# Seven block products for eight in a two-layer block's up projection, with the down projection as a stage of its own

## The chip, the core and the metric

The kernel runs on one core of one Trainium2 chip. The number that counts is the time of one execution in device microseconds (us). TensorE (PE) multiplies matrices, VectorE (DVE), ScalarE (ACT) and GpSimd (POOL) work elementwise, and SyncE (SP) issues most DMA transfers between DRAM and the on-chip memory SBUF. Each engine takes its instructions in order, so one that waits holds up all behind it. Matmul results land in PSUM, a small memory of eight banks.

## The reference

Two layers over 1024 tokens of width 1024, all in fp32. The change lies in the feed-forward part of the first, between its attention and the second layer:

```python
def conv_glu_ffn(h, w_up, w_conv, b_conv, w_down):
    z = h @ w_up                                   # 1024 x 1024 by 1024 x 5632
    zp = jnp.pad(z, ((0, 0), (1, 1), (0, 0)))      # three neighbouring tokens
    z = zp[:, :-2] * w_conv[0] + zp[:, 1:-1] * w_conv[1] + zp[:, 2:] * w_conv[2] + b_conv
    a, b = jnp.split(z, 2, axis=-1)                # 2816 channels each
    return (jax.nn.silu(a) * b) @ w_down           # 2816 x 1024
...
h = rmsnorm(x, g_norm2[l]) * (1.0 + sc2) + sh2
x = x + gt2 * conv_glu_ffn(h, w_up[l], w_conv[l], b_conv[l], w_down[l])
```

## The kernel before

Every fp32 product is made of three matmuls on a rounded type: a value is split into a high part (a cast on ACT) and a rest (a subtraction on DVE), and `mm3` multiplies high by high, rest by high and high by rest (L166 to L168 in the profile). `split` is that pair, with its lines L79 and L81.

The 2816 gated channels are 22 tiles of 128. Tile m has two weight tiles of `w_up`, one for `a` and one for `b`. `up_tile` multiplies one of them by all tokens: two halves of 512 tokens, eight blocks of 128 in the contracted width, three matmuls each, so 48 matmuls of 128x512 for a weight tile and 44 x 48 = 2112 in all. The result stays in PSUM (`up`), from where ACT (L1019) and two DVE instructions (L1020, L1022) make the three-token filter. ACT makes the SiLU of `a` (L1043), DVE the product with `b` (L1050), which is split into `gh` and `gl`. `down_w` loads the rows of `w_down` that belong to the tile, multiplies them by the gate row `gt2` on POOL (L992) and splits them.

After two such tiles `down` adds their part of the down projection: eight blocks of 128 tokens, two halves of 512 columns, 2 x 3 matmuls each, and a DVE addition into the rows `x2` (L1006). That is 96 matmuls for a group of two tiles and 11 x 96 = 1056 in all. `x2`, eight tiles of 512 KB, and `gt2` stay in SBUF throughout. The down groups are written in between the up tiles, so PE goes from one to the other. The next weight tile is loaded and split one tile ahead by `weights` and `w_next` along a list, `weight_order`, which runs on through the second layer.

In front of this the last two output-projection halves are interleaved with the normalised and transposed tokens 0 to 511 (`h_first`); `norm2(1)` and `to_act(xn[1], ...)` do the same for tokens 512 to 1023 while the first two up tiles multiply tokens 0 to 511. The transposed, split tokens are `h2T` (`h2h`, `h2l`). Behind it, `first_tokens` starts the second layer's input.

Of the kernel before, what the change touches and what calls it, by code (L numbers as in the profile page):

```python
# [6 lines left out]
F32 = mybir.dt.float32  # L7
# [289 lines left out]

def load_columns(cx, I):  # L300


# [30 lines left out]

def first_layer(cx, I, specs, x4_scr):
    nc = cx.nc
    tt = nc.vector.tensor_tensor
    ts = nc.vector.tensor_scalar
# [626 lines left out]
    def out_last():  # L966
        for n in range(2):
            yield from out_half(2 + n, ws[n], 1)
            if n == 0:
                cx.w_next()  # L970
                cx.w_next()
# [9 lines left out]
    wc = [cx.col["w_conv0"], cx.col["w_conv1"], cx.col["w_conv2"]]  # L981
    bc = cx.col["b_conv"]
    gt2 = gates[1]

    def down_w(m):
        hi = cx.pg("wdh", dt=F32R)
        lo = []
        for j in range(2):
            s = slice(j * 512, j * 512 + 512)
            f = cx.ge("wdf")  # L990
            nc.sync.dma_start(f, w_down[m * P:(m + 1) * P, s])
            nc.gpsimd.tensor_tensor(out=f, in0=f, in1=gt2[:, s], op=ALU.mult)  # L992
            lo.append(cx.hp("wdl", dt=F32R))
            cx.split(hi[:, s], lo[j], f)
        return hi, lo

    def down(gs, dws, rows=range(8), after=None):
        for i in rows:
# [12 lines left out]
    def up_tile(m, part):
        w = cx.weights(m > 0)
        c = m + NF * part
        S = cx.ps("S", "up", w=1024)
        for b in range(2):
            yield from cx.gemm_ch(S[:, b * 512:b * 512 + 512], h2T, w, b)
            yield 1.3
        y = cx.pg("y")
        nc.scalar.activation(y, S, AF.Identity, scale=wc[1][:, c:c + 1], bias=bc[:, c:c + 1])  # L1019
        stt(out=y[:, 1:], in0=S[:, :1023], scalar=wc[0][:, c:c + 1], in1=y[:, 1:],  # L1020
            op0=ALU.mult, op1=ALU.add)
        stt(out=y[:, :1023], in0=S[:, 1:], scalar=wc[2][:, c:c + 1], in1=y[:, :1023],  # L1022
            op0=ALU.mult, op1=ALU.add)
        return y

    def run(gen):
        while True:
            try:
                next(gen)
            except StopIteration as e:  # L1030
                return e.value

    pend_down, gs, dws = None, [], []
    for m in range(NF):
        ups = [up_tile(m, part) for part in range(2)]
        if m == 0:
            for u in ups:
                drain(half(u))
            drain(cx.to_act(xn[1], h2T, 1, a2, sh2))
        ya = run(ups[0])  # L1040
        if m == 0:
            cx.w_next()
        nc.scalar.activation(ya, ya, AF.Silu)  # L1043
        if pend_down is not None and m < NF - GRP:
            drain(down(*pend_down))
            pend_down = None
        yb = run(ups[1])
        if m == 0:
            cx.w_next()
        tt(out=ya, in0=ya, in1=yb, op=ALU.mult)  # L1050
        gs.append((cx.pg("gh", dt=F32R), cx.pg("gl", dt=F32R)))
        cx.split(*gs[-1], ya)
        dws.append(down_w(m))
        if len(gs) == GRP and m < NF - 1:
            pend_down, gs, dws = (gs, dws), [], []

# [821 lines left out]

def scratch(nc):
    d = lambda n, s: nc.dram_tensor(n, s, F32, kind="Internal").ap()  # L1880
    return {"x4": d("scr_x4", (1024, 1024)), "da": d("scr_da", (P, P)), "fc": d("scr_fc", (P, P)),
            "xs": d("scr_xs", (1024, 1024)), "ys": d("scr_ys", (1024, 1024)), "ya": d("scr_ya", (1024, 1024)),
            "t1": d("scr_t1", (1024, 1024)),
            "g0": d("scr_g0", (1024, 1024)), "g1": d("scr_g1", (1024, 1024))}


def weight_order(cx, I):

    w_in, w_in2 = I["w_in"][0], I["w_in_2"][0]
# [3 lines left out]
    order += [(I["w_out"][0], c, 256, "pg" if c % 512 else "wp") for c in range(0, 1024, 256)]  # L1893
    order += [(I["w_up"][0], (m + NF * part) * P, P, "wp") for m in range(NF)
              for part in range(2)]
    order += [(w_in2, c, 256, "wp", *what[1]) if kind == "v" else (w_in2, c, P, "wp")
              for kind, c, what in second_tasks()]
# [37 lines left out]
```

## Time and profile before

| | |
|---|---|
| three runs | 2695.33, 2696.01 (median), 2696.12 us |
| the profiled execution | 2694.87 us |
| its span, first to last instruction | 2693.0 us |
| up projection, first to last matmul start | 559.3 to 1239.2 us |
| down projection, first to last addition | 622.5 to 1293.1 us |

Busy time is a share of the span. The starts of matmuls, one after the other, tell PE's pace; the duration of one (389 ns) is longer, since neighbours overlap.

### The profile page before, as it was taken

What the parts mean: (1) busy time and instruction counts of PE and PEld (TensorE: products, weight loads), DVE (VectorE), ACT (ScalarE), POOL (GpSimd) and SP (SyncE); (2) the same over time, 40 slices, a digit from 0 to 9 for tenths busy, and PEclk for the clock granted to TensorE, in tenths of its full rate; (3) what the DMA queues carried; (4) which work ended last, traced back from release to release, by engine and by line L of the source; (5) the groups of instructions that cost most, each with busy time, mean ns of one, the idle gap of its engine ahead of it and who ended that gap; (6) DMA issues with size and microseconds to landing.
All of it is one profiled execution on the core that took longest, in us unless ns stands there. A gap on an engine that the chain in (4) does not pass through costs nothing. (4 is left out here: it accounts for less than half of the span.)

```text
span 2693.0 us, 38385 instructions
## 1 busy us (share of the span) xinstructions
PE 2626.4 (98%) x15391; PEld 2208.2 (82%) x15391; DVE 1547.2 (57%) x2857; ACT 1014.4 (38%) x1753; POOL 391.3 (15%) x368
## 2 busy tenths in 40 slices
PE   5999999999999999999899999999999999999999
PEld 5998667988888888887687777888888888888899
DVE  6645776665555555555577887554554544474443
ACT  4434776142222222223444444343343433352222
POOL 2211210431111111112202212310110100110000
PEclk9999999999999999999999999999999999999999
DMA  7111213421111111111123333222222222253532
GB/s 250 39 55 48 67 44 105 127 67 47 47 48 54 47 48 54 49 51 65 56 86 97 94 102 103 82 65 62 75 87 56 70 84 60 71 196 118 176 126 114
DMA packets 225439, 221.56 MB, mean 82 GB/s; under 512 B 15109, under 2 KB 173421, under 8 KB 225261
## 3 DMA queue, kind: packets, MB, share of 16 engines
q1 hardware_dynamic: 224608, 218.60, 26.4%
q8 instruction: 121, 1.98, 0.3%
q10 hardware_dynamic: 652, 0.51, 0.1%
q14 instruction: 58, 0.47, 0.1%
HBM read 180.67 MB, written 34.21 MB: 80 GB/s over the span
## 5 line engine op out<-in xcount | busy, mean ns | idle before, releaser
L81 DVE TENSOR_TENSOR wlo<-land,wh 128x1024 fp32r<-128x1024 f32 x161 | 209.1, 1300 | 323.5 <-ACT wh L79 322.7
L79 ACT CAST wh<-land 128x1024 fp32r<-128x1024 f32 x163 | 170.9, 1050 | 570.7 <-PE up L167 344.4
L166 PE MATMUL up<-h2h,wh 128*128 128x512 f32 x704 | 273.9, 390 | 0.7 <-DVE y L1022 0.7
L167 PE MATMUL up<-h2l,wh 128*128 128x512 f32 x704 | 274.1, 389 | 0.0
L168 PE MATMUL up<-h2h,wlo 128*128 128x512 f32 x704 | 273.9, 389 | 0.0
L1006 DVE TENSOR_TENSOR x<-dn,x 128x512 f32<-128x512 f32 x176 | 119.2, 688 | 75.5 <-PE dn L168 75.5
L1560 POOL TENSOR_TENSOR prob<-fc,consts 128x128 f32<-128x128 f32 x128 | 68.6, 555 | 635.1 <-PE pT L1600 278.3
L103 POOL TENSOR_TENSOR rstd<-ms,mhalf 128x1 f32<-128x1 f32 (+3 forms) x58 | 76.0, 1310 | 579.1 <-DVE ms L101 579.1
L89 ACT COPY pf<-pT 128x512 f32<-128x512 f32 (+1 forms) x208 | 114.0, 560 | 116.3 <-PE pT L1600 79.2
L166 PE MATMUL ag<-h3h,wh 128*128 128x512 f32 x384 | 156.9, 408 | 0.0
L992 POOL TENSOR_TENSOR wdf<-wdf,gate 128x512 f32<-128x512 f32 x44 | 73.4, 1690 | 568.5 <-DMA wdf<-in_w_down_dram 556.8
L166 PEld LDWEIGHTS up<-h2h,wh 128*128 128x128 f32 x704 | 132.1, 188 | 28.5 <-issue 1.1
L167 PEld LDWEIGHTS up<-h2l,wh 128*128 128x128 f32 x704 | 132.1, 188 | 27.7 <-DVE h2l L228 0.4
L168 PEld LDWEIGHTS up<-h2h,wlo 128*128 128x128 f32 x704 | 132.1, 188 | 27.5
L1580 ACT ACTIVATE prob<-prob,m 128x128 f32<-128x128 f32 (+7 forms) x128 | 99.4, 777 | 140.6 <-DVE m L1574 139.7
L168 PE MATMUL ag<-h3h,wlo 128*128 128x512 f32 x384 | 150.6, 392 | 0.0
L167 PE MATMUL ag<-h3l,wh 128*128 128x512 f32 x384 | 150.1, 391 | 0.0
L166 PE MATMUL dn<-wdh,gh 128*128 128x512 f32 x352 | 138.2, 393 | 1.7 <-DVE x L1006 1.5
L167 PE MATMUL dn<-wdl,gh 128*128 128x512 f32 x352 | 137.4, 390 | 0.0
L168 PE MATMUL dn<-wdh,gl 128*128 128x512 f32 x352 | 137.1, 389 | 0.0
L166 PE MATMUL tok<-wh,h1h 128*128 128x256 f32 x448 | 130.5, 291 | 2.7 <-ACT h1h L226 2.7
L168 PE MATMUL tok<-wh,h1l 128*128 128x256 f32 x448 | 128.7, 288 | 0.8 <-DVE h1l L228 0.8
(348 smaller groups left out, 6967.0 us busy)
## 6 DMA issues: line engine op xcount, KB each, us to landing
land<-in_w_in_dram SPq DMA_DIRECT2D x87, 512.0 KB, 4.0
wada<-in_w_ada_dram SPq DMA_DIRECT2D x96, 256.0 KB, 3.6
land<-in_w_up_dram SPq DMA_DIRECT2D x44, 512.0 KB, 3.9
wdf<-in_w_down_dram SPq DMA_DIRECT2D x44, 256.0 KB
scr_g<-gt SPq DMA_DIRECT2D x34, 256.0 KB, 3.5
x<-in_x_dram SPq DMA_DIRECT2D x16, 512.0 KB, 5.8
land<-in_w_out_dram SPq DMA_DIRECT2D x16, 512.0 KB
dab<-scr_da SPq DMA_DIRECT2D x32, 256.0 KB, 4.5
```

The costliest lines, as they stand in the source:

```text
L79: i = self.nc.scalar.copy(hi, src)
L81: eng.tensor_tensor(out=lo, in0=src, in1=hi.bitcast(F32), op=ALU.subtract)
L89: self.nc.scalar.copy(dst, src)
L103: self.nc.gpsimd.tensor_tensor(out=r[:, :width], in0=t[:, :width], in1=self.mhalf[:, :width], op=ALU.pow)
L166: i = mm(out, lh, rh, start=first, stop=False, **kw)
L167: mm(out, lh, rl, start=False, stop=False, **kw)
L168: self.last = mm(out, ll, rh, start=False, stop=last, **kw)
L992: nc.gpsimd.tensor_tensor(out=f, in0=f, in1=gt2[:, s], op=ALU.mult)
L1006: tt(out=x2[i][:, s], in0=o, in1=x2[i][:, s], op=ALU.add)
L1560: nc.gpsimd.tensor_tensor(out=pt[:, qs], in0=fc[:, qs], in1=cx.pos_q, op=ALU.add)
L1580: nc.scalar.activation(pt[:, :W], pt[:, :W], AF.Exp, bias=top, scale=-1.0, accum_out=rs)
```

## The change

The up projection of a pair of weight tiles (tile m of `a` and of `b`) is a product of a 2 x 2 matrix of blocks (two weight tiles by two halves of the contracted width) and another (the halves of that width by the two halves of the tokens). The class `Pairs` makes it of seven block products instead of eight. Each is 4 x 3 = 12 matmuls of 128x512, so a pair takes 84 instead of 96 and the stage 22 x 84 = 1848. For this POOL forms four sums of weight blocks in each pair (`sums`), ACT and DVE split seven (`split`), and two copies on ACT and five additions on DVE put the products together (`take`), from PSUM into SBUF tiles `z`. The filter, now in `gated`, reads `z`. The sums of token blocks (`T1` to `T4`, `B22`) are formed once ahead of the loop by `blocks(k)`, k = 0 to 3, on ACT, DVE and POOL; only the four products of tiles 0 and 1 that need tokens 0 to 511 alone come before it.

The product `a * b` goes to DRAM (`scr["g"]`), and so do `x2` and `gt2` ahead of the stage. The down projection follows when the up projection is over: its pools reuse the memory, `x2` and `gt2` are loaded back, and `load_group` brings each group's gate products and `w_down` rows. Its matmuls are as many as before. PSUM is divided anew in each stage.

```diff
+SEVEN = [("A11", "B11", "X"), ("S2", "T2", "Y"), ("A12", "B21", "X"), ("S3", "T3", "Z"),
+         ("S1", "T1", "W"), ("-A22", "T4", "Z"), ("S4", "B22", "W")]
...
+    def step(self, n, j, z, between=lambda: None):
+        if j == 0:
+            self.load(n + 2)
+        self.product(n, j)
+        self.sums(n + 1, j)
+        self.split(n + 1, j)
+        between()
+        self.take(n, j, z)
...
-    norm2(1)
...
+        for e in range(2):
+            ts(out=xh[j, e], in0=x_[:, e * 512:e * 512 + 512], scalar1=r, scalar2=None,
+               op0=ALU.mult)
+    for i in range(8):
+        nc.sync.dma_start(scr["x2"][i * P:(i + 1) * P, :], x2[i])
+    nc.sync.dma_start(scr["gt2"], gates[1][0:1, :])
+    psum.close()
+    yield
...
+    def blocks(k):
+        f = cx.pg("bf", (P, 2, 512))
+        o = cx.pg("bo", (P, 2, 512))
+        for e in range(2):
+            kk_ = k + 4 * e
+            t = cx.ps("T", "tr")
+            for j in range(4):
+                nc.tensor.transpose(t[:, j * P:(j + 1) * P], xh[j, e][:, k * P:(k + 1) * P],
+                                    cx.ident)
+            nc.scalar.activation(f[:, e], t, AF.Identity, scale=a2[:, kk_:kk_ + 1],
+                                 bias=sh2[:, kk_:kk_ + 1])
+            h, l = h2T(kk_, 0)
+            nc.gpsimd.tensor_tensor(out=o[:, e], in0=h.bitcast(F32), in1=l.bitcast(F32),
+                                    op=ALU.add)
+        cx.split(*b_new("B22", k, 0), f[:, 1])
+        t1, t3 = cx.t("sf", "t1", (P, 512)), cx.t("sf", "t3", (P, 512))
+        tt(out=t1, in0=f[:, 0], in1=o[:, 0], op=ALU.subtract)
+        nc.gpsimd.tensor_tensor(out=t3, in0=f[:, 1], in1=f[:, 0], op=ALU.subtract)
+        t2 = f[:, 0]
+        tt(out=t2, in0=f[:, 1], in1=t1, op=ALU.subtract)
+        cx.split(*b_new("T2", k, 0), t2)
+        cx.split(*b_new("T3", k, 0), t3)
+        cx.split(*b_new("T1", k, 0), t1)
+        tt(out=o[:, 1], in0=t2, in1=o[:, 1], op=ALU.subtract)
+        cx.split(*b_new("T4", k, 0), o[:, 1])
...
+    for m in range(2):
+        for j in (0, 2):
+            up.product(m, j)
+            up.take(m, j, z_of(m))
...
+    for k in range(4):
+        blocks(k)
...
+        tt(out=y[0], in0=y[0], in1=y[1], op=ALU.mult)
+        nc.sync.dma_start(scr["g"][m * P:(m + 1) * P, :], y[0])
...
+    psum.enter_context(cx.psum("psd", S=2, T=3, V=1))
+    cx.plan(second_weights(cx, I))
+    gt2 = cx.pg("gate")
+    cx.bcast_row(gt2, scr["gt2"][0])
+    x2 = []
+    for i in range(8):
+        t = cx.pg("x2")
+        nc.sync.dma_start(t, scr["x2"][i * P:(i + 1) * P, :])
+        x2.append(t)
...
+    def load_group(q):
+        g, w = [], []
+        for m in range(GRP * q, GRP * q + GRP):
+            gh, gl = cx.pg("gh", dt=F32R), cx.pg("gl", dt=F32R)
+            nc.sync.dma_start(gl.bitcast(F32), scr["g"][m * P:(m + 1) * P, :])
...
+                nc.sync.dma_start(f, w_down[m * P:(m + 1) * P, j * 512:j * 512 + 512])
...
+    for q in range(1, NF // GRP - 1):
+        gen = group(q)
+        drain(down(*cur, range(0, 3)))
+        nxt = next(gen)
+        drain(down(*cur, range(3, 8)))
```

Three places where the order of instructions differs. SP at the start of the stage, before (weight tiles of the up projection follow those of the output projection, `land`; `wada` are weights of the modulation):

```order
L125 DMA land_5443<-in_w_out_dram 128x4x256
L125 DMA land_5445<-in_w_out_dram 128x4x256
L362 DMA wada_5574<-in_w_ada_dram 128x512
L125 DMA land_5597<-in_w_up_dram 128x8x128
L125 DMA land_5978<-in_w_up_dram 128x8x128
L125 DMA land_5984<-in_w_up_dram 128x8x128
```

and after (`scr_gt` and `scr_x` are the stores of `gt2` and `x2`, `pairs` the raw weights of one pair, two transfers of 512 KB):

```order
L473 DMA wada_5577<-in_w_ada_dram 128x512
L1098 DMA scr_gt<-gate_5421 1x1024
L1097 DMA scr_x<-x_975_4557 128x1024
L1097 DMA scr_x<-x_976_4559 128x1024
L1097 DMA scr_x<-x_977_4561 128x1024
L1097 DMA scr_x<-x_978_4563 128x1024
L1097 DMA scr_x<-x_1077_4928 128x1024
L1097 DMA scr_x<-x_1078_4930 128x1024
L1097 DMA scr_x<-x_1079_4932 128x1024
L1097 DMA scr_x<-x_1080_4934 128x1024
L323 DMA pairs_6233<-in_w_up_dram 128x8x128 x2
L323 DMA pairs_6236<-in_w_up_dram 128x8x128 x2
```

The first `w_up` weights now stand on SP behind all eight stores of `x2`.

SP at the end of the up projection, before (weights of up and down in turn):

```order
L991 DMA wdf_10050<-in_w_down_dram 128x512
L991 DMA wdf_10181<-in_w_down_dram 128x512
L125 DMA land_9795<-in_w_up_dram 128x8x128
L125 DMA land_9983<-in_w_up_dram 128x8x128
L991 DMA wdf_10187<-in_w_down_dram 128x512
```

and after (the first row is the last gate product's store, the last row the first gate product's load):

```order
L1172 DMA scr_gate<-y_9694 128x1024
L125 DMA land_9709<-in_w_in_dram 128x8x128
L252 DMA gate_9711<-scr_gt 128x1024
L1227 DMA x_2012_9713<-scr_x 128x1024
L1227 DMA x_2013_9715<-scr_x 128x1024
L1227 DMA x_2014_9717<-scr_x 128x1024
L1227 DMA x_2015_9719<-scr_x 128x1024
L1227 DMA x_2016_9721<-scr_x 128x1024
L1227 DMA x_2017_9723<-scr_x 128x1024
L1227 DMA x_2018_9725<-scr_x 128x1024
L1227 DMA x_2019_9727<-scr_x 128x1024
L1237 DMA gl_9730<-scr_gate 128x1024
```

Ten loads of 512 KB stand between the last store and the first load that the down projection multiplies.

DVE in a down group, before (the additions into `x2` run without a break):

```order
L1006 TENSOR_TENSOR x_976_4556<-dn_6651,x_976_4556 128x512
L1006 TENSOR_TENSOR x_976_4556<-dn_6659,x_976_4556 128x512
L1006 TENSOR_TENSOR x_977_4558<-dn_6667,x_977_4558 128x512
L1006 TENSOR_TENSOR x_977_4558<-dn_6675,x_977_4558 128x512
L1006 TENSOR_TENSOR x_978_4560<-dn_6683,x_978_4560 128x512
```

and after (`gl` and `wdl` are the rests of the next group's gate products and weights):

```order
L1266 TENSOR_TENSOR x_2012_9713<-dn_9949,x_2012_9713 128x512
L1266 TENSOR_TENSOR x_2012_9713<-dn_9957,x_2012_9713 128x512
L1250 TENSOR_TENSOR gl_9930<-gl_9930,gh_9929 128x1024
L1266 TENSOR_TENSOR x_2013_9715<-dn_9965,x_2013_9715 128x512
L81 TENSOR_TENSOR wdl_9933<-wdf_9935,wdh_9932 128x512
L1266 TENSOR_TENSOR x_2013_9715<-dn_9973,x_2013_9715 128x512
L81 TENSOR_TENSOR wdl_9934<-wdf_9937,wdh_9932 128x512
L1266 TENSOR_TENSOR x_2014_9717<-dn_9981,x_2014_9717 128x512
L1250 TENSOR_TENSOR gl_9940<-gl_9940,gh_9939 128x1024
L1266 TENSOR_TENSOR x_2014_9717<-dn_9989,x_2014_9717 128x512
L81 TENSOR_TENSOR wdl_9943<-wdf_9945,wdh_9942 128x512
L81 TENSOR_TENSOR wdl_9944<-wdf_9947,wdh_9942 128x512
```

The next group's splits, which wait for its loads, now stand between the additions that empty PSUM.

## Rows read from the trace of the kernel before

**Rows 1.** The page's first part: busy time of the engines, their share of the span, and instructions.

```profile
PE 2626.4 (98%) x15391; PEld 2208.2 (82%) x15391; DVE 1547.2 (57%) x2857; ACT 1014.4 (38%) x1753; POOL 391.3 (15%) x368
```

**Rows 2.** Stretches of the span (from:to, length): busy time and instructions of PE, weight load, DVE, ACT and POOL, then the granted clock as a share of 2.4 GHz, DMA share, GB/s. First the start of the stage, its middle and its end.

```profile
560.00:600.00 40.00, 39.23 (x187) 31.99 (x186) 28.05 (x37) 23.60 (x34) 12.58 (x14) 1.00 0.24 73
700.00:1200.00 500.00, 500.00 (x2207) 413.84 (x2206) 255.22 (x271) 114.28 (x122) 51.48 (x30) 1.00 0.16 48
1245.00:1300.00 55.00, 50.70 (x228) 39.18 (x228) 37.50 (x77) 24.08 (x41) 24.60 (x21) 1.00 0.20 77
```

**Rows 3.** PE in order of time inside the stage (start, duration, line, operation, out<-in).

```profile
699.80 0.39 PE L168 MATMUL dn<-wdh,gl 128*128 128x512 f32 x1
700.03 0.39 PE L166 MATMUL dn<-wdh,gh 128*128 128x512 f32 x1
...
701.84 0.39 PE L168 MATMUL dn<-wdh,gl 128*128 128x512 f32 x1
```

**Rows 4.** Groups of instructions between 700 and 1200 us (line, operation, shape, count, busy time, mean ns of one, idle time before them).

```profile
L1006 DVE TENSOR_TENSOR x<-dn,x 128x512 f32<-128x512 f32 x118 | 80.2, 689 | 59.9 <-PE dn L168 59.9
L992 POOL TENSOR_TENSOR wdf<-wdf,gate 128x512 f32<-128x512 f32 x30 | 51.5, 1737 | 448.9 <-DMA wdf<-in_w_down_dram 448.9
...
L1022 DVE SCALAR_TENSOR_TENSOR y<-up,cols,y 128x1023 f32<-128x1023 f32 x31 | 39.7, 1281 | 0.8
L1020 DVE SCALAR_TENSOR_TENSOR y<-up,cols,y 128x1023 f32<-128x1023 f32 x31 | 39.5, 1275 | 0.0
L1019 ACT ACTIVATE y<-up,cols,cols 128x1024 f32<-128x1024 f32 x31 | 37.4, 1206 | 0.0
...
L81 DVE TENSOR_TENSOR wdl<-wdf,wdh 128x512 fp32r<-128x512 f32 x30 | 19.3, 684 | 0.0
L1050 DVE TENSOR_TENSOR y<-y,y 128x1024 f32<-128x1024 f32 x15 | 18.4, 1226 | 0.5
L81 DVE TENSOR_TENSOR gl<-y,gh 128x1024 fp32r<-128x1024 f32 x15 | 18.4, 1225 | 16.7 <-ACT gh L79 16.7
L79 ACT CAST wdh<-wdf 128x512 fp32r<-128x512 f32 x30 | 17.1, 617 | 0.0
L1043 ACT ACTIVATE y<-y 128x1024 f32<-128x1024 f32 x15 | 15.9, 1061 | 52.9 <-DVE y L1022 52.9
L79 ACT CAST gh<-y 128x1024 fp32r<-128x1024 f32 x15 | 15.8, 1050 | 59.4 <-DVE y L1050 59.4
```

**Rows 5.** PE in order of time where the output projection (`tok`) ends and the up projection begins; eight transposes lie between.

```profile
558.42 0.28 PE L168 MATMUL tok<-wh,mixl 128*128 128x256 f32 x1
558.54 1.04 PE L205 MATMUL tr<-consts,xn 128*128 128x128 f32 x8
559.33 0.48 PE L166 MATMUL up<-h2h,wh 128*128 128x512 f32 x1
```

**Rows 6.** POOL, DVE and ACT at that place in order of time, with the idle time before in brackets: the last additions into `x2`, a subtraction beside them and one without them, the last normalised row, and the activation behind a transpose.

```profile
559.35 3.29 POOL L937 TENSOR_TENSOR x<-og,x 128x256 f32<-128x256 f32 x4 [9.43 <-DVE og L936]
580.05 7.27 POOL L992 TENSOR_TENSOR wdf<-wdf,gate 128x512 f32<-128x512 f32 x5 [11.73 <-DVE h2l L228]
```

```profile
561.02 1.01 DVE L228 TENSOR_TENSOR h2l<-trf,h2h 128x512 fp32r<-128x512 f32 x1
...
563.85 0.69 DVE L228 TENSOR_TENSOR h2l<-trf,h2h 128x512 fp32r<-128x512 f32 x1
...
568.36 0.75 DVE L241 TENSOR_SCALAR xn<-x,rstd 128x1024 f32<-128x1024 f32 x1 [0.66 <-POOL rstd L103]
```

```profile
559.61 0.78 ACT L225 ACTIVATE trf<-tr,sh,a 128x512 f32<-128x512 f32 x1 [1.47 <-PE tr L205]
```

**Rows 7.** The two stretches in which DMA is saturated, columns as in rows 2.

```profile
15.00:40.00 25.00, 10.26 (x44) 8.23 (x43) 23.69 (x32) 6.39 (x9) 9.29 (x6) 1.00 1.09 347
...
2380.00:2400.00 20.00, 20.00 (x136) 15.78 (x132) 13.17 (x27) 14.26 (x29) 2.93 (x4) 1.00 1.05 373
```

**Rows 8.** Kinds of DMA issue (out<-in, queue, count, KB each, median us from issue to landing).

```profile
land<-in_w_up_dram SPq DMA_DIRECT2D x44, 512.0 KB, 3.9
...
x<-scr_x SPq DMA_DIRECT2D x8, 512.0 KB, 7.1
```

**Rows 9.** Stretches at the end of the one long stop of PE, columns as in rows 2, and PE in order of time at its end.

```profile
1312.00:1316.00 4.00, 0.00 (x0) 0.00 (x0) 0.00 (x0) 0.53 (x2) 0.00 (x0) 0.50 0.09 6
1316.00:1320.00 4.00, 2.42 (x8) 1.83 (x9) 2.61 (x4) 2.59 (x5) 0.00 (x0) 0.50 0.00 0
1320.00:1324.00 4.00, 4.00 (x23) 3.00 (x23) 0.81 (x2) 1.20 (x3) 0.00 (x0) 0.90 0.00 0
```

```profile
1317.58 1.12 PE L205 MATMUL tr<-consts,xn 128*128 128x128 f32 x4 [9.79 <-DVE h3l L215]
...
1319.35 0.63 PE L1169 MATMUL dt<-h3h,wdt 128*112 128x512 f32 x1
1319.78 0.63 PE L1172 MATMUL dt<-h3l,wdt 128*48 128x512 f32 x1
...
1320.95 0.39 PE L1169 MATMUL dt<-h3h,wdt 128*112 128x512 f32 x1
1321.18 0.39 PE L1172 MATMUL dt<-h3l,wdt 128*48 128x512 f32 x1
```

**Rows 10.** PE's waits between 1236 and 1345 us (engine, tile, line, for whom: us in total, times, longest).

```profile
PE dn L166 <- DVE x L1006: 1.5, 3, 0.5
```

More of the change, by code (lines that the diff above doesn't have):

```diff
@@ L331, in load_columns, with first_layer @@
         yield
[L336 removed]
+def first_layer(cx, I, scr):
+    specs = weight_order(cx, I)
+    x4_scr = scr["x4"]
     nc = cx.nc
@@ new lines, in first_layer, with b_new @@
+    nc.sync.dma_start(scr["gt2"], gates[1][0:1, :])
+    psum.close()
+    yield
+    psum.enter_context(cx.psum("psu", S=5, T=3))
+    wc = [cx.col["w_conv0"], cx.col["w_conv1"], cx.col["w_conv2"]]
+    bc = cx.col["b_conv"]
+    bt = {}
+    def b_new(nm, k, n):
+        tag = "act2" if len(bt) < 12 else "act"
+        bt[nm, k] = tuple(cx.t(tag, nm, (P, 512), F32R) for _ in range(2))
+        return bt[nm, k]
+    B = {nm: (lambda k, nm=nm: bt[nm, k]) for nm in ("B22", "T1", "T2", "T3", "T4")}
@@ new lines, in first_layer @@
+    for m in range(2):
+        up.load(m)
+    for m in range(2):
+        for j in (0, 2):
+            up.split(m, j)
+    up.sums(0, 0)
+    for m in range(2):
+        for j in (0, 2):
+            up.product(m, j)
+            up.take(m, j, z_of(m))
+    for j in (1, 3):
+        up.sums(0, j + 1)
+        up.split(0, j)
+    for k in range(4):
+        blocks(k)
+    for j in (4, 5, 6):
+        up.split(0, j)
+    up.load(2)
+    post = iter(())
+    for m in range(NF):
+        for j in range(7):
+            between = lambda: next(post, None)
+            if m < 2 and j in (0, 2):
+                if m == 1:
+                    up.sums(m + 1, j)
+                    up.split(m + 1, j)
+                else:
+                    up.sums(m + 1, j)
+                continue
+            if m == 0:
+                up.product(m, j)
+                up.sums(m + 1, j)
+                up.split(m + 1, j)
+                up.take(m, j, z_of(m))
+            else:
+                up.step(m, j, z_of(m), between)
+        drain(post)
+        up.load(m + 2)
+        post = gated(m)
@@ L1009, in down, with group @@
             yield 2.6
[L1011 to L1041, printed above, removed]
-            cx.w_next()
[L1043 to L1055, printed above, removed]
+    def group(q):
+        gen = load_group(q)
+        next(gen)
+        return gen
+    gen = group(0)
+    cur = next(gen)
+    for q in range(1, NF // GRP - 1):
[3 more added lines that the diff above has]
+        drain(down(*cur, range(3, 8)))
+        if q in (5, 6):
+            cx.w_next()
+        cur = nxt
+    pend_down = cur
+    gs, dws = next(group(NF // GRP - 1))
     gf = cx.pg("g_final")
@@ L1887, in weight_order, with second_weights @@
 def weight_order(cx, I):
-    w_in, w_in2 = I["w_in"][0], I["w_in_2"][0]
+    w_in = I["w_in"][0]
     cols = [512, 0, 256, 1280, 768, 1536, 1024]
     order = [(w_in, c, 256, "pg" if n % 2 else "wp") for n, c in enumerate(cols)]
[L1893 to L1896, printed above, removed]
+    return order + [(I["w_out"][0], c, 256, "pg" if c % 512 else "wp")
+                    for c in range(0, 1024, 256)]
+def second_weights(cx, I):
+    w_in2 = I["w_in_2"][0]
+    order = [(w_in2, c, 256, "wp", *what[1]) if kind == "v" else (w_in2, c, P, "wp")
               for kind, c, what in second_tasks()]
@@ L1907, in both_layers @@
         scr = scratch(cx.nc)
-        with cx.pool("all", act=32, wl=2, wp=4, pg=21, hp=9, ge=5):
-            h3T, late = first_layer(cx, I, weight_order(cx, I), scr["x4"])
-            second_layer(cx, I, h3T, late, scr, out[0])
+        first = first_layer(cx, I, scr)
+        with cx.pool("all", act=32):
+            with cx.pool("one", wl=2, wp=4, pg=21, hp=9, ge=5):
+                next(first)
+            with cx.pool("up", act2=24, pl=2, sf=4, wx=16, pg=6, hp=4):
+                next(first)
+            with cx.pool("two", wl=2, wp=4, pg=21, hp=9, ge=5):
+                h3T, late = next(first)
+                second_layer(cx, I, h3T, late, scr, out[0])
 def kernel(**inputs):
```

149 lines of the change are left out of this document (130 added, 19 removed).

## The prediction

> **What bounds the kernel now.** I read the page's shares first, then the stretches of the stage, then PE in order of time, then the groups by shape. PE is busy 98% of the span and nothing else comes near [rows 1]. Between 700 and 1200 us PE has 500.00 of 500 us, 2207 matmuls at full clock, while DVE has 255, ACT 114, POOL 51 and DMA a share of 0.16 [rows 2]. Two matmuls of 128x512 start 0.2266 us apart (2.04 us for nine) [rows 3], and 500/2207 is the same. So in this stage a matmul less is 0.2266 us less, as long as PE stays fed, and every us without work for PE is one us more. The start of the stage loses 0.77 us of 40, the end 4.3 of 55 [rows 2]: before, the seams cost next to nothing, because the first up tiles cover the second norm and the down groups lie between up tiles.
>
> **What is removed.** 2112 - 1848 = 264 matmuls x 0.2266 = 59.8 us. The down projection keeps its 1056. The 0.8 us of idle time at the stage's start and part of what is lost at its end go too; I credit 1 us.
>
> **The loop of pairs.** PE needs 84 x 0.2266 = 19.03 us for a pair. DVE has seven splits of 0.684, five additions like those into x2 of 0.689, two filters each of 1.275 and 1.281 and a product of 1.226 [rows 4]: 4.79 + 3.45 + 5.11 + 1.23 = 14.6 us. ACT has seven casts and two copies of about 0.617, two activations of 1.206 and a SiLU of 1.061: 9.0. POOL has four sums of the size of L992, 1.737 each: 6.9. A product lasts 12 x 0.2266 = 2.7 us, and the second product into a bank begins one product after the take that frees it, so a take of 0.7 us has some 2 us in hand. I take the loop as bound by PE, at no further cost.
>
> Against that speaks a row: a subtraction that takes 0.69 us took 1.01 beside POOL's additions [rows 6]. Of DVE's 14.6 us, 11.1 (splits, filters, product) read two operands from SBUF. If 46% more falls on the part beside POOL (6.9 of 19.03), DVE needs 14.6 + 11.1 x 0.36 x 0.46 = 16.5, still under PE. At the far end, with no overlap at all, 14.6 + 6.9 = 21.5 and the loop costs 22 x 2.5 = 55 us more. I take the row's rate.
>
> The Trainium skill says the same against this change: GPSIMD Engine Reference, section Specifications, has POOL share its SBUF interfaces with VectorE and contend with DVE instructions that have two SBUF inputs. The filters read PSUM before and SBUF now, so by that rule more of DVE's work is exposed; this trace agrees as far as the one subtraction of 1.01 us goes, and shows no filter from SBUF.
>
> **First stop: output projection to loop.** The last output matmuls end at 559.3 [rows 5]. POOL finishes x2 at 562.6 [rows 6]. SP holds the eight stores of x2 ahead of every load of w_up; rows 4 to 7 can be stored only after that, 4 x 0.524 MB, then comes 1.05 MB for pair 0. These 3.15 MB at the 347 GB/s of a saturated stretch [rows 7] are 9.1 us, and they begin at about 561: the first weights are there at about 570, those of pair 1 three us later. Before, the first up matmul started at 559.33 [rows 5]. Only four products, 48 matmuls, can run now (10.9 us). Each second one waits for a copy on ACT that stands behind casts of POOL's first sums (570 + 3 x 1.7 = 575), so they end at about 586.
>
> The activations of the transposed tokens (0.78 each [rows 6]) stand on ACT behind the last of these copies, so the first block sums get their input at about 587.6. POOL's list from 570: four sums, three tokens' restorations (to 582), a wait until 587.6, nine block operations (to 603) and four sums for pair 1 (to 610). DVE's list from 588: eight instructions for each of four blocks, about ten splits and three additions, 45 x 0.69 = 31 us, to 619. PE has by then done 92 matmuls (20.9 us) and 32 transposes (3.2, at 0.79 for eight [rows 5]). 619 - 559.3 - 24 is 35 us without work. At the least (DVE keeps up with POOL, end at 610) it is 27; at the most (DVE's subtractions at 1.01 throughout) 45. I take 35, by the row without disturbance, since POOL waits for part of the time.
>
> **Second stop: up to down.** Let T0 be the end of the last product. Then follow on DVE and ACT one addition 0.69, one activation 1.21, two filters 2.56, SiLU 1.06, product 1.23: 6.75 us, with handovers 7.5 to 8. Only then can SP issue the last gate store, and behind it, in order, one weight tile, the gate row, eight tiles of x2 and then the first gate products: with these two and four halves of w_down 7.3 MB, 21 us at 347 GB/s. The first gate tile is there at T0 + 28, everything at T0 + 31. POOL scales the weights (4 x 1.74), ACT casts (0.617), DVE subtracts (0.684): first matmul at T0 + 31, PE dense from T0 + 36.8, with some 14 matmuls (3.2 us) of the first tile done. That is 34 us. In before a load of x2 rows in a burst of eight took 7.1 us to land, against 3.9 for a single weight tile [rows 8], so queueing is what such bursts do. Bounds: 27, if the ten loads in front start at T0 (they need only memory that is free before the last filter) and 46, if the first group's splits go one after the other.
>
> Clock: after PE's 9.8 us stop before, the granted clock was 0.50, so 1.2 GHz, and matmuls started 0.43 us apart for the first 3 us of work before they came 0.23 apart [rows 9]. Each stop costs some 1.5 to 2 us more of half speed once work is dense; 2 in all at the second, 2 at the first: 4.
>
> **The down stage.** A group is 96 matmuls, 21.8 us, with 16 additions of 0.689, two splits of 1.225 and four of 0.684 on DVE: 16.2 us. Before, the additions ran alone, and PE waited for them 1.5 us in all [rows 10]. Now a group's gate loads are issued as the buffers of the last but one come free, about 1 us before the current group starts, and land 4 us or more later [rows 8]. On DVE the split of 1.2 us stands behind block 0's additions (3.4 us into the group) and cannot start before landing and a cast of 1.05, at about 4.6. The additions behind it fall 1.8 us late, and a second split follows; with three PSUM banks for 1.36 us halves PE waits 0.5 to 2 us in a group. Nine such groups: 4.5 to 18, and I take 10 by the sum of DVE's list. The last group begins without cover for its loads in the second layer's interleaving: 0 to 3, I take 1.
>
> **Sum.** -59.8 - 1 + 35 + 34 + 4 + 10 + 1 = +23.2 us. The profiled execution took 2694.87 us, which gives 2718; that execution is 1.1 us under the median, so a median may read 2719.
>
> **Rivals.**
> (a) The first stop is half as long and the second at its lower bound. Mechanism: ACT gets to the transposed tokens before POOL runs out of work, and POOL goes at 1.45 us (five in 7.27 [rows 6]), so its twenty operations run from 570 to 599 without a wait and DVE keeps pace: 599 - 559.3 - 24 = 16. With 27 at the second, 3 of clock and 9 in the down stage with its tail the sum is -59.8 - 1 + 16 + 27 + 3 + 9 = -6: 2689. It decides where both stops together come to under 48 us. For it: POOL was idle 85% of the span. Against: ACT's order puts the activations behind the last copy.
> (b) DVE, slowed by POOL, becomes the bound of the loop. From 19.03 us on for a pair each us costs 22: at 20 us +21, at the far end +55. Time 2740 to 2773, about 2750. For it the 1.01 us row; against it 2.5 us of margin at that row's rate.
> (c) Each down group waits for its gate loads in full: landing 7.1 us as in the burst, then cast and split, some 4 us of PE in each of nine groups, 36 for 10: 2744.
> (d) The change does not do what it says: the 264 matmuls go but each of the three products per pair that add to a bank waits 0.5 us for its copy or addition, 22 x 1.5 = 33 more: 2751. Against: 2 us in hand.
>
> **How the numbers follow.** Forecast 0.54, (a) 0.18, (b) 0.11, (c) 0.11, (d) 0.06. Of the time, less than 0.2% (5.4 us) can't be told from no change. (a) is split evenly between faster and the same; the forecast's own lower bounds (27 + 27 + 4 and no late additions make about -1) lend 0.03 to the same. So faster 0.09, same 0.12, slower 0.79. The forecast's own range is 2703 to 2735; to leave out no more than 2 in 10 the range goes from 2690, (a), to 2752, the middle of (b) and (d).
>
> **What would show it.** PE starts 0.2266 us apart and no idle time in the loop, with pairs 19.0 us apart: the saving. Two stretches in which PE has little work, 60 us from 560 and 37 us where the up projection ends (at about 619 + 1756 x 0.2266 = 1017), with the granted clock at 0.5 in them: the stops. In the first, PE waits at its end for DVE's splits of T2, T3 and T1; in the second for DVE's wdl and gl, behind DMA gl and wdf. In the down stage waits of dn for the additions into x2, 10 us in all. The forecast is wrong if pairs come over 19.5 us apart, if either stop is under 25 us, or if the down groups come over 24 us apart.

## The result, and the profile after

The changed kernel took 2723.14 us (median of 4 runs, 2721.15 to 2726.04), before 2695.67 on the same chip: a ratio of 1.0104, with an interval of 1.0087 to 1.0122. That is 27.5 us slower; the forecast was 23 slower, at 2718, with a range of 2690 to 2752. The profiled execution took 2724.39 us with a span of 2722.6; before's span was 2693.0. One of e3's four executions below took 2906.72 us at a mean granted clock of 0.843 and is left out of that run's median.

The page's first part of the kernel after, which answers to [rows 1]:

```profile
PE 2591.5 (95%) x15127; PEld 2169.5 (80%) x15127; DVE 1711.6 (63%) x3101; ACT 1096.8 (40%) x1923; POOL 534.2 (20%) x468
```

PE has exactly 264 instructions less and 35 us less busy time, and yet the span is 29.6 us longer: its share falls from 98 to 95%. Where it stands idle is seen in the stretches, columns as in [rows 2]:

```profile
560.00:570.00 10.00, 4.48 (x14) 2.38 (x14) 6.56 (x18) 6.18 (x12) 4.12 (x7) 0.61 1.04 325
570.00:590.00 20.00, 15.15 (x64) 10.99 (x62) 14.07 (x12) 9.29 (x16) 14.61 (x10) 0.94 0.39 100
590.00:620.00 30.00, 18.05 (x43) 11.75 (x44) 26.69 (x31) 14.16 (x25) 15.50 (x11) 0.66 0.00 0
620.00:640.00 20.00, 17.53 (x70) 13.78 (x69) 20.00 (x22) 7.57 (x13) 12.59 (x8) 0.93 0.20 53
700.00:1000.00 300.00, 300.00 (x1325) 248.42 (x1324) 229.26 (x269) 138.47 (x190) 91.75 (x61) 1.00 0.26 79
1020.00:1060.00 40.00, 9.52 (x29) 6.10 (x27) 17.35 (x13) 9.70 (x11) 8.97 (x5) 0.58 0.64 234
1060.00:1100.00 40.00, 38.43 (x159) 30.61 (x160) 32.34 (x42) 8.96 (x13) 18.81 (x13) 0.95 0.45 140
```

In the loop of pairs PE is busy 300.00 of 300 us at full clock, 300/1325 = 0.2264 us a matmul: nothing of the saving is lost there. It is given back in the two stops. PE's waits (tile and line, for whom: us in total, times, longest), in the first stop from 555 to 660 us, in the second from 1010 to 1070, and in the down stage from 1070 to 1400:

```profile
PE w L167 <- DVE T L81: 7.4, 2, 3.8
PE tr L1135 <- DVE xh L1094: 6.2, 4, 4.2
PE w L166 <- ACT T L79: 3.4, 1, 3.4
PE w L166 <- ACT wxh L79: 2.6, 2, 2.2
PE w L166 <- DVE u L375: 2.5, 1, 2.5
PE tr L1135 <- ACT bf L1137: 1.9, 2, 1.4
PE w L166 <- ACT m L379: 1.8, 2, 1.2
```

```profile
PE dn L166 <- ACT wdh L79: 30.2, 2, 28.8
PE dn L167 <- DVE wdl L81: 1.0, 1, 1.0
```

```profile
PE tr L205 <- DVE h3l L215: 11.0, 3, 9.8
PE dn L166 <- DVE x L1266: 8.4, 9, 3.0
```

The waits of the first stop add to 25.8 us, those of the second to 31.2. More is lost than that, since what PE does in between runs at the low clock (0.66 and 0.58 granted). From PE in order of time: the output projection's transposes start at 557.91 and end about 558.7, the last product and the first down matmul are these rows (start, duration, idle time before in brackets):

```profile
1023.82 0.39 PE L168 MATMUL w<-B,wxl 128*128 128x512 f32 x1
1053.00 0.80 PE L166 MATMUL dn<-wdh,gh 128*128 128x512 f32 x1 [28.79 <-ACT wdh L79]
```

So the up stage lasts 1024.2 - 558.7 = 465.5 us for 1848 x 0.2266 + 3.2 = 422 us of work: 43 lost. From 1024.2 to 1100 are 75.8 us; 169 down matmuls (10 before 1060, 159 after) are 38.3 of them: 37 lost. The sum with the saving is -59.8 - 1 + 43 + 37 + 8 (PE's waits of `dn` for `x`) = +27. From the end of the output projection to the last down matmul the two traces differ by 732.2 to 759.4, +27.2 us. Some 3 us more stand in the second layer, which the change doesn't touch: what follows the last down matmul took 1401.5 us in before and 1404.5 in after, but also 1398.8 to 1405.4 in e1, e3, e4, e5 and e7 below, which leave it as it is, so this part is within the scatter of such runs.

The 9.8 us wait for `h3l` in the third list of waits is the stop of [rows 9], unchanged.

### The profile page after: what moved, and what is told of

Same layout as the page of the kernel before. It is cut to its first block, busy times and chain, and to the rows that moved or that the text cites. A ratio compares the mean times of both kernels' runs of the same rounds, so it can differ in the third digit from the quotient of the medians.

```text
span 2722.6 us, 38908 instructions
## 1 busy us (share of the span) xinstructions
PE 2591.5 (95%) x15127; PEld 2169.5 (80%) x15127; DVE 1711.6 (63%) x3101; ACT 1096.8 (40%) x1923; POOL 534.2 (20%) x468
## 5 line engine op out<-in xcount | busy, mean ns | idle before, releaser
L79 ACT CAST wh<-land 128x1024 fp32r<-128x1024 f32 x119 | 124.5, 1048 | 226.6 <-PE ag L167 49.2
L81 DVE TENSOR_TENSOR wlo<-land,wh 128x1024 fp32r<-128x1024 f32 x117 | 144.7, 1238 | 111.3 <-ACT wh L79 110.8
L166 PE MATMUL w<-T,wxh 128*128 128x512 f32 x352 | 140.2, 399 | 8.1 <-ACT T L79 3.4
L167 PE MATMUL w<-T,wxh 128*128 128x512 f32 x352 | 140.6, 400 | 7.4 <-DVE T L81 7.4
L168 PE MATMUL w<-T,wxl 128*128 128x512 f32 x352 | 139.6, 398 | 0.0
L167 PE MATMUL tok<-wlo,h1h 128*128 128x256 f32 x448 | 129.4, 289 | 0.5 <-DVE ms L101 0.5
L166 PEld LDWEIGHTS dn<-wdh,gh 128*128 128x128 f32 x352 | 67.2, 191 | 57.9 <-ACT wdh L79 31.1
L166 PE MATMUL gt<-h3h,wh 128*128 128x512 f32 x272 | 111.4, 410 | 0.0
L168 PE MATMUL gt<-h3h,wlo 128*128 128x512 f32 x272 | 106.7, 392 | 0.0
```

Source lines behind the costliest of these rows:

```text
L79: i = self.nc.scalar.copy(hi, src)
L81: eng.tensor_tensor(out=lo, in0=src, in1=hi.bitcast(F32), op=ALU.subtract)
L166: i = mm(out, lh, rh, start=first, stop=False, **kw)
L167: mm(out, lh, rl, start=False, stop=False, **kw)
L168: self.last = mm(out, ll, rh, start=False, stop=last, **kw)
```

## The experiments

Every time below is set against after's 2723.14 us; each ratio is against before, run on the same chip. A first stop or second stop is that of the prediction; T0 is the end of the last product. The runs were made on three chips, on which before took 2694.95 us (beside e1 to e4), 2694.36 (e5 to e8) and 2695.25 (e9, e10), so up to 1.3 us of a difference to after may be the chip's. The first column of the table is the label.

| run | what | median us | ratio and interval | to after |
|---|---|---|---|---|
| e1_dup | one product made twice | 2781.80 | 1.0324, 1.0307 to 1.0342 | +58.7 |
| e2_group0_first | first gate loads ahead of `x2` rows | 2716.79 | 1.0083, 1.0068 to 1.0098 | -6.3 |
| e3_store_act | last gate store on ACT's queue | 2720.07 | 1.0094, 1.0077 to 1.0111 | -3.1 |
| e4_blocks_dve | POOL's block operations on DVE | 2716.65 | 1.0080, 1.0065 to 1.0095 | -6.5 |
| e5_blocks_early | two blocks ahead of the first products | 2718.60 | 1.0082, 1.0065 to 1.0098 | -4.5 |
| e6_stop2 | second stop shortened | 2707.62 | 1.0046, 1.0031 to 1.0061 | -15.5 |
| e7_stop1 | first stop shortened | 2712.44 | 1.0064, 1.0049 to 1.0079 | -10.7 |
| e8_both_stops | e6 and e7 | 2698.29 | 1.0013, 1.0003 to 1.0022 | -24.9 |
| e9_store_late | e8, store behind the loads | 2693.72 | 0.9994, 0.9985 to 1.0003 | -29.4 |
| e10_sums_dve | e9, first sums on DVE | 2689.92 | 0.9980, 0.9970 to 0.9989 | -33.2 |

**e1_dup: is a product worth its matmuls?** The eighth product comes back, as a repetition of the product of S3 and T3.

```diff
+        if j == 3:
+            for k in range(4):
+                self.cx.mm3(self.x[n, bank], (h[:, k], l[:, k]), self.B[bn](k), k == 0,
+                            k == 3, skip_group_check=True)
```

> In each of the 22 pairs the product S3*T3 is made twice, the second time over the first: 22 x 12 = 264 matmuls more, as many as the change removes, and nothing else. Theory (the loop of pairs is bound by PE, so the 264 matmuls were really saved and the seams gave them back): +59.8 us against the changed kernel, about 2783 us, pairs 21.75 us apart. Rival (the loop is near another bound, DVE beside POOL): the extra matmuls hide in part, under +45 us. Half is right if pairs come 21.75 us apart but the total moves otherwise.

It cost 58.7 us, and the first down matmul came 58.4 later (1111.4 for 1053.0). The saving of 59.8 is real, and the loop is PE's. DVE's busy time from 700 to 1000 fell from 229.26 to 198.51, since pairs come more slowly. PE's waits for additions in the down stage came to 11.8 us here, for 8.4.

**e2_group0_first and e3_store_act: what is the second stop made of?** In e2 the gate row and group 0's loads go ahead of the eight `x2` rows and the second layer's tile; in e3 only the last gate product's store goes to ACT's queue.

```diff
-    cx.plan(second_weights(cx, I))
-    x2 = []
-    for i in range(8):
-        t = cx.pg("x2")
-        nc.sync.dma_start(t, scr["x2"][i * P:(i + 1) * P, :])
-        x2.append(t)
...
     gen = group(0)
+    x2 = []
+    for i in range(8):
+        t = cx.pg("x2")
+        nc.sync.dma_start(t, scr["x2"][i * P:(i + 1) * P, :])
+        x2.append(t)
+    cx.plan(second_weights(cx, I))
```

```diff
-        nc.sync.dma_start(scr["g"][m * P:(m + 1) * P, :], y[0])
+        (nc.scalar if m == NF - 1 else nc.sync).dma_start(scr["g"][m * P:(m + 1) * P, :], y[0])
```

> Only the order of SP's loads at the second stop: gate row and the first down group's gate products and weights ahead of the eight x2 rows and the weight tile of the second layer. Theory (the queue of ten transfers in front is the larger part of the second stop): the first down matmul comes some 17 us after the last product instead of 29, and the time falls by 11 to 13 us, to about 2711. Rival (the chain of scaling on POOL and splits on DVE sets the restart, or the wait for x2 in the additions takes the place of the queue): under 5 us less.

> Only the last gate product's store goes out on ACT's queue instead of SP's, so that SP's reloads no longer stand behind the last pair's filter chain. Theory: reloads begin at once after the last product instead of 8 us later, the time falls by 7 us, to about 2716. Rival (the reloads wait for memory that the filter chain still holds): 0 to 2 us less.

e2's first down matmul came at T0 + 17.2, as the order of SP's queue would have it, for 28.8: that the loads in front make 11.6 us of the stop is shown. But the time gained only 6.3, for the 11 to 13 of the theory: half came back in the down stage (PE's waits there and one row of DVE in order of time):

```profile
PE dn L166 <- DVE x L1260: 14.6, 12, 5.7
```

```profile
1056.23 1.23 DVE L81 TENSOR_TENSOR wlo<-land,wh 128x1024 fp32r<-128x1024 f32 x1 [6.31 <-ACT wh L79]
```

The split of the second layer's weights, whose load was now the last of the burst, made DVE idle for 6.3 us with additions into `x2` queued behind it, and PE ran out of banks. The stop had moved, and e6 must hold this split back too.

e3 fell short, with 3.1 us for the 7 of its theory and a first down matmul at T0 + 23.4, because SP still stood. SP's queue in after and then in e3, in order of time (start, time that the issues took), and SP's waits in e3 between 1015 and 1042 us:

```profile
1033.76 5.24 SPq L1227 DMA_DIRECT2D x<-scr_x  x8
```

```profile
1020.96 14.87 SPq L1227 DMA_DIRECT2D x<-scr_x  x8
1035.87 0.44 SPq L1237 DMA_DIRECT2D gl<-scr_gate  x1
```

```profile
SPq L1227 <- DVE y L1166: 6.4, 1, 6.4
SPq L1227 <- DMA scr_gate<-y: 4.7, 1, 4.7
```

Eight issues that need 5.24 us took 14.87. One row stood until the last filter was done, the next until the store on ACT's queue had landed, though it loads nothing of what is stored. That fits the cause that the rival named, memory that the filter chain still holds: the pool of the `x2` rows takes over the memory of the one before it, and by the trace's records the second row's load waits expressly for the store's completion counter. The loads begin earlier, but the first gate load gains only 4.1 us of issue, 1035.87 for 1039.97 in after, and 2.9 against T0, which was 1023.0 for 1024.2.

**e4_blocks_dve and e5_blocks_early: what is the first stop made of?** In e4 the twelve operations that POOL has in the four blocks go to DVE; in e5 blocks 0 and 1 are written ahead of the first four products.

```diff
-            nc.gpsimd.tensor_tensor(out=o[:, e], in0=h.bitcast(F32), in1=l.bitcast(F32),
+            nc.vector.tensor_tensor(out=o[:, e], in0=h.bitcast(F32), in1=l.bitcast(F32),
...
-        nc.gpsimd.tensor_tensor(out=t3, in0=f[:, 1], in1=f[:, 0], op=ALU.subtract)
+        nc.vector.tensor_tensor(out=t3, in0=f[:, 1], in1=f[:, 0], op=ALU.subtract)
```

```diff
     for m in range(2):
         up.load(m)
+    blocks(0)
     for m in range(2):
         for j in (0, 2):
             up.split(m, j)
+    blocks(1)
...
-    for k in range(4):
+    for k in (2, 3):
         blocks(k)
```

> Only the twelve block operations of POOL in the first stop (token restorations and T3) are made by DVE. Theory (in the first stop DVE and POOL hold each other up: DVE subtractions of 0.68 us took 1.74 beside POOL, and each block goes from one engine to the other): DVE gets 12 x 0.68 = 8 us more work but some thirteen of its instructions become 1.06 us shorter and the hand-overs go, the time falls by 6 to 12 us, to about 2714. Rival (DVE's list alone sets the end of the stop): 5 to 8 us more, about 2730.

> Only an order: the blocks k = 0 and 1 of the token sums are written ahead of the first four products, so that on ACT the activations of the transposed tokens no longer stand behind the copies of those products, and POOL restores their tokens before the weights land. Theory (the first stop is long because ACT's order holds the token sums back until 585): the sums begin some 15 us earlier, about half of them move under the wait for the weights, and the time falls by 8 to 12 us, to about 2713. Rival (the work of DVE and POOL between 570 and 620 is a sum that the order does not change, and the first products come later instead): 0 to 4 us less.

e4 gained 6.5, inside the theory's 6 to 12, by giving twelve more operations to the engine that already was the late one. Why, the two lists say. DVE in after, in order of time, and POOL beside it (its first row from a narrower window):

```profile
598.43 1.73 DVE L1144 TENSOR_TENSOR t<-bf,bo 128x512 f32<-128x512 f32 x1 [1.17 <-POOL bo L1140]
600.09 1.74 DVE L81 TENSOR_TENSOR T<-bf,T 128x512 fp32r<-128x512 f32 x1
601.75 0.68 DVE L1147 TENSOR_TENSOR bf<-bf,t 128x512 f32<-128x512 f32 x1
```

```profile
598.36 1.26 POOL L1140 TENSOR_TENSOR bo<-h2h,h2l 128x512 f32<-128x512 f32 x1
599.58 1.71 POOL L1145 TENSOR_TENSOR t<-bf 128x512 f32<-128x512 f32 x1
605.59 3.43 POOL L1140 TENSOR_TENSOR bo<-h2h,h2l 128x512 f32<-128x512 f32 x2 [4.30 <-DVE T L81]
```

DVE in e4, the same operations with the blocks' work all on DVE:

```profile
588.43 0.68 DVE L1151 TENSOR_TENSOR bo<-bf,bo 128x512 f32<-128x512 f32 x1
589.03 0.68 DVE L81 TENSOR_TENSOR T<-bf,T 128x512 fp32r<-128x512 f32 x1
589.63 0.68 DVE L1144 TENSOR_TENSOR t<-bf,bo 128x512 f32<-128x512 f32 x1
590.24 0.68 DVE L81 TENSOR_TENSOR T<-t,T 128x512 fp32r<-128x512 f32 x1
```

A DVE operation on two SBUF operands takes 0.68 us by itself and up to 1.74 beside a POOL operation. That is no rate of 46% more: the two engines take turns. POOL's restoration ran from 598.36 to 599.62. The DVE subtraction that started at 598.43 ended at 600.16, so its own 0.68 us began at 599.48, 0.14 before POOL was done; POOL's next operation, 1.28 us by itself, then took 1.71. What a meeting costs DVE is what is left of POOL's operation, whatever DVE's own length. The same holds for all 75 stretched DVE operations of this kind that before (545 to 1240 us) and after (568 to 1000 us) have: counted back from its end by its own length, each begins 0.04 to 0.24 us before a POOL operation ends.

The waits for T on DVE fell from 7.4 to 2.0 us, and T0 came at 1017.9 (1046.5 less 28.6). A new wait came with it: PE stood 5.5 us for `wxh`, because a sum on POOL got no turn beside DVE's now unbroken list. POOL in e4:

```profile
601.28 6.41 POOL L337 TENSOR_TENSOR sum<-pairs 128x512 f32<-128x512 f32 x1 [25.71 <-DVE T L81]
```

e4 takes away the turns, the hand-overs between the engines and POOL's slower operations together; it doesn't say how much of the 6.5 each is worth.

e5 gained 4.5, between its theory and its rival. The first product came later, at 573.7 for 569.3, as the rival had it, since the splits of the weights now stand among the blocks on DVE (PE waits 3.9 us for `wxl`). But less of the blocks was left after the products, and T0 came at 1019.4 for 1024.2. PE still waits for T and `u` of DVE, 5.6 us in all.

**e6_stop2 and e7_stop1: do the causes add up in one stop?** e6 joins e3 with the order of e2 (but the second layer's weight tile stays in front), puts `x2` rows 4 to 7 behind group 1's loads and holds the second layer's splits until groups 5 and 6. e7 joins e5 with an e4 that leaves the restorations of blocks 0 and 1 to POOL.

```diff
     gen = group(0)
+    load_rows(range(4))
...
         gen = group(q)
+        if q == 1:
+            load_rows(range(4, 8))
...
         if q in (5, 6):
+            cx.done[q - 7] = cx.last
             cx.w_next()
```

```diff
-            nc.gpsimd.tensor_tensor(out=o[:, e], in0=h.bitcast(F32), in1=l.bitcast(F32),
+            (nc.gpsimd if k < 2 else nc.vector).tensor_tensor(out=o[:, e], in0=h.bitcast(F32), in1=l.bitcast(F32),
```

> Second stop alone, three parts: the last store on ACT's queue, the first group's loads ahead of x2 (of which rows 4 to 7 come behind the second group's loads), and the two weight splits of the second layer held back to groups 5 and 6, since in the run with the first group's loads ahead DVE's additions stood 6 us behind such a split. Theory (the second stop is a queue of loads and what is put in front of the additions): first down matmul 12 to 15 us after the last product instead of 29, no new wait for x2, 15 to 18 us less than the changed kernel, about 2706. Rival (x2 is late instead, whatever the order, because the 7 MB must come anyway): 8 us less at the most, 2715.

> First stop alone: blocks 0 and 1 ahead of the first products, and of the twelve block operations POOL keeps only the four restorations that it can make before the weights land; the others are DVE's. Theory (order and the mutual hold-up of DVE and POOL add): 14 to 18 us less, about 2707. Rival (DVE's list is the bound and both edits get at the same time): no better than the better of the two alone, 7 to 10 us less, about 2715.

e6 gained 15.5 (14.2 against before beside it), the lower end of the theory's 15 to 18: PE's wait was 11.5 us for 28.8, and the down stage's waits stayed near those of after (10.5 for 8.4). e7 gained 10.7, which is e4 and e5 added (11.0) but less than the theory's 14 to 18. PE's longest waits in what remains are 8.0 us for `xh`, the normalised rows of tokens 512 to 1023 that the transposes need, and 5.0 for `wxh`, behind a sum on POOL that again got no turn until DVE's list paused. POOL in e7:

```profile
598.08 5.80 POOL L337 TENSOR_TENSOR sum<-pairs 128x512 f32<-128x512 f32 x1 [7.30 <-issue]
```

**e8_both_stops: are the two stops independent?**

> The edits at both stops together. Theory (the seams are independent and carry all that the 264 matmuls bring): the gains add, 29 to 36 us less, 2687 to 2694, at or under the kernel before (2695). Rival (what is taken from one stop comes back in the loop or in the down stage): 20 us less at the most, 2703.

24.9 us against 15.5 + 10.7 = 26.2 (against before beside them, 23.5 and 14.2 + 9.4): they add, but come to less than the theory's 29 to 36. Both stops are shown to cost at least what was won back in them, and the kernel is within 0.3% of before. What was left in the second stop is read from SP's queue in order of time, from ACT's, and from SP's waits between 1008 and 1034 us:

```profile
1014.05 14.01 SPq L1240 DMA_DIRECT2D wdf<-in_w_down_dram  x2
1028.10 2.10 SPq L1278 DMA_DIRECT2D x<-scr_x  x4
```

```profile
1025.07 0.36 ACTq L1172 DMA_DIRECT2D scr_gate<-y  x1
```

```profile
SPq L1240 <- DMA scr_gate<-y: 13.2, 1, 13.2
```

A weight half stood 13.2 us for the store on ACT's queue, which was issued at 1025.07.

**e9_store_late and e10_sums_dve: two more causes, taken one by one.** e9 multiplies the last gate product into two buffers of its own and lets SP store them behind the loads, and loads the second layer's first weight tile later. e10 makes the weight sums of pairs 0 and 1 on DVE, for in e8 a sum on POOL took 5.2 and 5.8 us beside DVE's full list.

```diff
+        if m == NF - 1:
+            for e in range(2):
+                s = slice(e * 512, e * 512 + 512)
+                last_y.append(cx.t("act", "ylast", (P, 512)))
+                tt(out=last_y[e], in0=y[0][:, s], in1=y[1][:, s], op=ALU.mult)
...
+            for e in range(2):
+                st = nc.sync.dma_start(scr["g"][(NF - 1) * P:NF * P, e * 512:e * 512 + 512],
+                                       last_y[e])
```

```diff
-        tt = self.cx.nc.gpsimd.tensor_tensor
+        tt = (self.cx.nc.vector if n < 2 else self.cx.nc.gpsimd).tensor_tensor
```

> Against the run with both stops edited: the last gate product goes to buffers of its own, and its store is issued by SP behind all loads that the restart needs (there, ACT's next casts stood behind its issue on ACT's queue until 1025, and SP's loads from the eighth on until 1028); the second layer's first weight tile is loaded later. Theory (in that run nothing but the store held ACT and SP): the first down matmul comes up to 8 us earlier, PE is dense 5 us earlier, 2691 to 2694. Rival (DVE's filter chain of the last pair, 9 us, is what the restart waits for in any case): 0 to 2 us less, 2697.

> The same and, at the first stop, the eight weight-block sums of pairs 0 and 1 on DVE instead of POOL, where single ones took 5.2 and 5.8 us beside DVE. Theory (POOL is held off by DVE's dense stream, and PE waits 5 us for the split of such a sum): 8 x 0.68 = 5.4 us more on DVE, but no wait for POOL: 3 to 6 us less than the run beside it. Rival (DVE's list is the bound of the first stop, so what is added there is added to the time): 2 to 5 us more.

e9 gained 4.6 on e8 (on another chip) and e10 3.8 more, both as their theories had the time. PE's wait at the second stop fell to 8.9 us in e9 for 11.7 in e8; of the up to 8 us foreseen for the first down matmul, 2.9 came. In e10 the wait for `wxh` is gone, and one of 4.1 us for T on ACT is new. e10 is faster than before by 0.2%, with an interval of 0.1 to 0.3%, which is some 5 us. Its stretches 560 to 620, 620 to 640 and 700 to 1000:

```profile
560.00:620.00 60.00, 45.00 (x170) 32.42 (x171) 56.13 (x86) 34.83 (x62) 16.29 (x14) 0.83 0.35 100
620.00:640.00 20.00, 18.05 (x79) 14.36 (x78) 19.33 (x21) 9.60 (x14) 7.39 (x5) 1.00 0.26 79
700.00:1000.00 300.00, 300.00 (x1325) 248.49 (x1324) 227.42 (x266) 137.10 (x186) 87.87 (x58) 1.00 0.25 76
```

PE has 170 instructions done from 560 to 620 us, where after had 14 + 64 + 43 = 121. In the loop PE's count is the same to the instruction. Not tried: to load the first weights ahead of the stores of `x2`, for which the buffers would have to be found; what that would gain is open, since the transposes that stand before the first product wait for `xh` until 568 in any case.

## Why the prediction was right, point by point

**The saving** was right: 264 matmuls at 0.2264 to 0.2266 us, 59.8 foreseen and 58.7 when one product per pair was put back.

**The loop** was right that it stays PE's, with 300.00 us of 300; rivals (b) and (d) fall. But how DVE is slowed was not. The term took 46% from one row, 1.01 for 0.69, as a rate on the share of time beside POOL. That row's operands lie in SBUF too (`trf` and `h2h`), and the turns explain it: the POOL addition in front of it is half as large and was nearly over, and 561.02 + 1.01 - 0.69 = 561.34 is again 0.15 ahead of its end (before, POOL):

```profile
560.75 0.74 POOL L937 TENSOR_TENSOR x<-og,x 128x256 f32<-128x256 f32 x1
```

The trace of before had the larger price as well, hidden in a mean of 1482 ns. Eight of these 31 subtractions, 1.225 us by themselves, took 2.14 to 2.37 beside a POOL operation of 128x512 (the group from 700 to 1200 us, one of the eight, and POOL beside it):

```profile
L81 DVE TENSOR_TENSOR wlo<-land,wh 128x1024 fp32r<-128x1024 f32 x31 | 45.9, 1482 | 167.2 <-ACT wh L79 167.2
728.97 2.17 DVE L81 TENSOR_TENSOR wlo<-land,wh 128x1024 fp32r<-128x1024 f32 x1 [2.34 <-ACT wh L79]
728.76 1.30 POOL L992 TENSOR_TENSOR wdf<-wdf,gate 128x512 f32<-128x512 f32 x1 [39.70 <-DMA wdf<-in_w_down_dram]
```

DVE's groups in the loop of after (count, busy time, mean ns, idle time before), 700 to 1000 us:

```profile
L1163 DVE SCALAR_TENSOR_TENSOR y<-z,cols,y 128x1023 f32<-128x1023 f32 x32 | 49.3, 1540 | 11.5 <-ACT y L1161 11.5
...
L1166 DVE SCALAR_TENSOR_TENSOR y<-z,cols,y 128x1023 f32<-128x1023 f32 x32 | 40.7, 1273 | 0.0
...
L81 DVE TENSOR_TENSOR wxl<-pairs,wxh 128x512 fp32r<-128x512 f32 x32 | 29.3, 914 | 0.0
...
L337 POOL TENSOR_TENSOR sum<-pairs 128x512 f32<-128x512 f32 x15 | 33.0, 2201 | 81.4 <-DVE wxl L81 81.4
```

One filter and one split of `pairs` in each pair bear it: of the 32 of each, 16 filters took 1.81 for 1.27 and 15 splits 1.18 for 0.68, which the means of 1540 and 914 mix. POOL bears it too, at 2201 for 1283 of the like sums. That is 1.0 us a pair, less than the 1.9 that the term allowed (its own factors give 16.4, for the 16.5 stated), because few of DVE's operations meet one of POOL's: a wrong rule came out on the safe side by luck. DVE is busy 229.26 us in the 15.8 pairs of 19.03 us that fit the stretch, 14.5 a pair (15.6 by the sum of the durations, as neighbours overlap by some 0.07 us), and PE's margin of 4.5 us covered it. In the first stop there was no margin.

**The first stop** was undersized: 35 and 2 for the clock foreseen, 43 measured, inside the term's own bounds of 27 to 45. Its shape was right: the four products end at 584 for 586, PE waits for T and is nearly dense from about 620 for 619. The step that failed is "45 x 0.69 = 31 us" for DVE's list, taken "by the row without disturbance". From 585 to 619 DVE did 33 instructions and not 45: ten were held up beside POOL, by 9.4 us in all, and DVE stood 2.4 us more for POOL's restorations. After 620 came a wait of 2.5 us for `u`, so that 70 instructions and not 88 fit into 620 to 640. What e4 won back of this is 6.5 us.

**The second stop** was right in sum and cause: 34 and 2 foreseen, 37 measured, T0 + 28.8 for T0 + 31. e2 shows that the loads ahead of the first gate load make 11.6 us of it, e3 and e9 that the last store has a share. The term's lower bound, ten loads that start at T0, was not to be had: in e3 a row still stood 6.4 us until the last filter was done, so not all of their memory is free before it.

**The clock** was foreseen at 4 us. Waits of 25.8 and 31.2 out of 43 and 37 leave 17 and 6 in which PE works slowly, in stretches of down to 0.61 and 0.58 granted. By the starts, 45 matmuls of the first stop and 17 of the second came at the lower level, 0.43 us apart for 0.23, which is some 9 and 3.5 us. So the sum came out by luck: the idle time was taken too long where the low clock was taken too short. In the first stop part of the slow work may stand beside DVE's list and cost nothing by itself; no run separates the two.

**The down stage** was foreseen at 11 with its tail and measured some 8; rival (c) falls with 8.4 us of waits in all. **Rival (a)**, both stops short, was wrong for this order of instructions, where the stops cost 43 and 37. e10 comes to its time, 2690 for 2689, but not by its split: counted in the same way, e10's stops still cost some 32 and 20 us, for its 16 and 27.

## What to carry to other kernels

When the middle of a stage is bound by PE, a matmul less is worth its pitch, but what must be paid is at the seams: ask for each stage that begins anew what its first instruction waits for, and count every issue, split and copy that is queued ahead of it. Here 60 us saved in the loop were lost at two seams, and moving a few loads, one store and some additions between queues and engines won 33 back, in steps that added up. Work that an idle POOL could do is not free to DVE where DVE's list is what PE waits for, and a group's mean hides it: look at the single rows where two engines meet.

## What the runs showed of the hardware that was not expected

- DVE and POOL take turns on operations with two operands in SBUF. A DVE operation that meets one of POOL's runs for its own length from some 0.14 us before POOL's end, so 0.68 us becomes up to 1.74 and 1.225 up to 2.37; 1.28 becomes 1.71 to 2.28 on POOL, and up to 6.4 (e4) where DVE's list has no gap. DVE's additions with one operand in PSUM stayed at 0.68 to 0.69 through the loop, also the 15 that lay wholly beside a POOL sum.
- A DMA issue on SP can stand until a store on ACT's queue is done, 13.2 us in e8, where the two share no data. The program gives its DMAs eight completion counters in turn: in the trace's records of e8 the store carries counter 102, and the load that stood is the next with 102 and waits for it. Moving the store behind the loads in e9 took the wait away. The 4.7 us in e3 are another thing: that load carries counter 99 and waits for 102 expressly, which fits memory that the store still reads.
